# Ordering six of eight experts by token count on the chip, with one overflow loop instead of two

## The chip, the cores and the metric

The kernel runs on one core of a Trainium2 chip. The metric is device time in microseconds (us) of one execution; lower is better. The kernel before took 1444.34 us (median of three runs, 1441.13 to 1444.92).

## What is computed

A two-layer decoder block over 256 tokens of width 1024. Layer 0 is a retention layer with a dense SwiGLU, layer 1 a sparse attention with a mixture of experts. All of the change lies in the mixture and in the sum and norm behind it:

```python
logits = x @ w_router                        # 256 x 8
top_v, top_i = top_k(logits, 2); w = softmax(top_v)
gate = sum(one_hot(top_i, 8) * w[..., None], axis=1)
for e in range(8):                           # D 1024, inner width 3584
    a, b = split(x @ w_in[e], 2)
    out = out + gate[:, e:e+1] * ((silu(a) * b) @ w_out[e])
x = layer_norm(alpha * x + out)
```

The weights are float32. Each expert has 44 MB of them and each is read once, so the eight experts read 352 MB.

## The kernel before, in words

**Weights.** The host lays each expert's weights out as 21 blocks of 2 MB ("slots", 128 rows of 16 KB): 14 of `w_in` (`moe_a`) and 7 of `w_out` (`moe_o`). A slot holds two raws of 1 MB. `load` (from L193) gives each slot a place and issues one transfer on SP's queue: in the ring (eight raws, so four slots), in `more` (one slot) or in `ext` (three). So eight slots, 16 MB, can be on their way or in use. A slot is loaded when the slot that held its place has been used (`release`, `load_next`); the order of the loads is the order of use.

**The order of an expert.** The loop `for e in range(NE)` takes the experts in their order 0 to 7, each in four stages s. A stage multiplies the gathered tokens with its part of `w_in` (`w_in`, matmuls of L1239; four slots, two in stage 3), then does the previous stage's product with `w_out` (`w_out`, matmuls of L1301; two slots, one for stage 3), and then transposes this stage's hidden values (`h_transpose`, L1279). The last `w_out` of an expert so falls into stage 0 of the next one. Behind that stage stands the scatter of the finished expert into X3 (`scatter`, L1343 and L1353), behind stage 1 the transposes of the selection matrix (L1182). Experts 2j and 2j+1 share one selection matrix and one gather (`build_S`, `gather`).

**Groups and the branch.** The tokens of an expert stand in up to 96 places, in three groups of 32 (NG = 3). Groups 0 and 1 are always multiplied (`first`). Group 2 is multiplied only if the expert has more than 64 tokens:

```python
with tc.If(M["n", e] > 64) as cmp:
    for j in (i, i + 1):
        mm(j, us[j][1], (2,))
```

Otherwise `zero` (L1226) clears the bank with four small matmuls, five times per expert: once in each stage's `w_in` and once in the first `w_out`. In this text an expert with group 2 is heavy, one without is light. The count is read into a register of the matmul engine by `count`.

**The end.** Behind the last `h_transpose`, `sum_open` (L1385) starts the last sum: four matmuls with the identity bring X3 into four PSUM banks. Then come the last `w_out`, the split of its result on ACT and DVE (L1327, L1328), the scatter matmuls (L1343) and the norm with the output (`last_out`). `gbr`, the norm's factors, is loaded behind the last weights. For more than 96 tokens of an expert there are two overflow loops (`overflow`, L1448), for places 97 to 224 and from 225; on these inputs both loops run no round, so only their reads of the trip count and their branches are executed.

**Names that the change touches.** `M["rg"]` holds rank and gate of each token by expert, `M["cni"]` and `M["cnf"]` the counts as integers and as floats, `C` a table from the host, `zb` a tile of zeros, `bank(tag)` one of four PSUM banks of the tag "mm" or of "acc".

Of the kernel before, what the change touches and what calls it, by code (L numbers as in the profile page):

```python
# [37 lines left out]
LOOK = 3  # L38


def _tables():
    c = np.zeros((128, 1056), np.float32)
# [65 lines left out]
def tile_decoder(ctx, tc, x, ret_w_in, ret_gn_g, ret_w_out, nsa_w_kv, cmp_k_pe, cmp_k_w1, cmp_k_w2,  # L108
# [17 lines left out]
    C = sb.tile([128, 1056 - 384], F32, name="C")  # L126
# [66 lines left out]
    def load(z):  # L193
# [11 lines left out]
        for i, r in enumerate(z.raws):  # L205
            r.ap = ap[:, i * 2048:(i + 1) * 2048]
            for view, src in r.parts:
                nc.sync.dma_start(view(r.ap), src)
# [858 lines left out]
    if stop not in ("r1", "r2", "r3"):  # L1067
# [64 lines left out]
        def moe_gates():  # L1132
# [13 lines left out]
            trip = sb.tile([128, 2], I32, name="trip")  # L1146
            for i in range(2):
                nc.vector.tensor_scalar(trip[:, i:i + 1], mc, cap + i * 128 + 0.5, float(NE), op0=ALU.is_gt,
                                        op1=ALU.mult)
            M["trip"] = trip  # L1150

        def build_S(j):
# [5 lines left out]
            rg = M["rg"]  # L1158
# [52 lines left out]

        def units_m(w, e, i, n):

            us = []
            for j in range(0, n, 2):
                rs = [raw() for _ in range(2)]
                Slot(rs, w[e, (i + j) // 2])
                us.extend([Unit(r, lambda a: a, conv=False) for _ in range(2)] for r in rs)
            return us
# [4 lines left out]
        def zero(ps):  # L1224
            for q in range(4):
                nc.tensor.matmul(ps[q * 32:(q + 1) * 32], zb[:, 0:32], zb, start=True, stop=True,  # L1226
                                 skip_group_check=True)
# [43 lines left out]
        def h_transpose(s):  # L1271
            def f():
                nch = ws(s) // 128
                hT = ptile([128, NG, 2, 128], F32, "hT")
                for gs, tag in (((0, 1), "acc"), ((2,), "mm")):
# [14 lines left out]
        def w_out(e, s, us):  # L1290
# [41 lines left out]
            for i, u in enumerate(us):  # L1332
                step([u[0]], first(i, u[0]), look=0)
                if i % 2:
# [71 lines left out]
        zb = sb.tile([128, 512], BF16, name="zb")  # L1406
# [8 lines left out]
        for e in range(NE):  # L1415
            step([], count(e), look=0)
            for s in range(4):
                nl, nb = (8, 4) if s < 3 else (4, 2)
                w_in(e, s, units_m(wst['moe_a'], e, 8 * s, nl))
                if prev:  # L1420
                    w_out(*prev)
                step([], h_transpose(s), look=0)
                if s == 0:
                    step([], transpose_S(e) if e == 0 else scatter(e - 1), look=0)
                    if e == 0:
                        step([], moe_gates, look=0)
                if s == 1 and e:
# [8 lines left out]
        step([], sum_open, look=0)  # L1436
# [9 lines left out]
        def overflow(i):  # L1446

            n = nc.values_load(M["trip"][0:1, i:i + 1], min_val=0, max_val=NE)  # L1448
            open_phase("over")
            with tc.For_i(0, n, 1) as ev:  # L1450
                col = ptile([128, 2, NT, 1], F32, "ocol")
                nc.vector.tensor_copy(col, M["rg"][:, :, :, bass.ds(ev, 1)])
                nc.vector.tensor_scalar(col[:, 0], col[:, 0], -float(cap + 128 * i), None, op0=ALU.add)
                xf = ptile([128, NT, D], F32, "oxf")
                nc.vector.tensor_add(xf, M["xh"].bitcast(F32), M["xl"].bitcast(F32))
                Sm = ptile([128, NT, 128], F32, "oS")
                for t in range(NT):
                    nc.vector.tensor_scalar(Sm[:, t], iota1, col[:, 0, t], None, op0=ALU.is_equal)
                ps = bank()
                for t in range(NT):  # L1460
                    nc.tensor.transpose(ps[:, tsl[t]], Sm[:, t], ident)
                SmT = ptile([128, S], F32, "oST")
                nc.scalar.copy(SmT, ps[:, 0:256])
                xg = ptile([128, KD, 128], F32, "oxg")
                for kq in range(2):
                    ps = bank()
                    for k in range(4):
                        kk = kq * 4 + k
                        for t in range(NT):
                            nc.tensor.matmul(ps[:, k * 128:(k + 1) * 128], xf[:, t, kk * 128:(kk + 1) * 128],  # L1470
                                             Sm[:, t], start=k == 0 and t == 0, stop=t == 1, skip_group_check=True)
                    nc.scalar.copy(xg[:, kq * 4:kq * 4 + 4], ps.rearrange("p (k n) -> p k n", k=4))
                y = [bank("acc") for _ in range(2)]
                wi_e = moe_w_in[0, bass.ds(ev, 1)].rearrange("o (k p) n -> p (o k) n", p=128)
                wo_e = moe_w_out[0, bass.ds(ev, 1)].rearrange("o (c p) n -> p (o c) n", p=128)
                for g in range(FFE // 256):
                    ab = bank()
# [160 lines left out]
```

## Time and profile before

| | |
|---|---|
| median of three runs | 1444.34 us (1441.13 to 1444.92) |
| the profiled execution's own time | 1444.41 us |
| its span in the trace | 1442.5 us |
| matmul engine (PE) busy | 1354.2 us, 94% |
| vector engine (DVE), scalar engine (ACT) | 471.3 us (33%), 346.8 us (24%) |
| moved by transfers | 450.78 MB, mean 313 GB/s |
| mean granted clock of PE | 0.982 of 2.4 GHz |

A profile shows one execution. PE is the matmul engine and PEld its weight loads, DVE, ACT and POOL are the vector, scalar and general engines, SP issues the transfers. A letter q behind an engine means its sequencer. "L1239" is a line of the kernel. A line of the timeline gives start, duration, engine, line, operation, output and inputs, how many instructions are merged (x), and in brackets the idle time before with what ended it. A float32 matmul shows as two records. The mixture's weights stream from about 600 us to the end, so the last 840 us of the span are the stage that counts here.

### The profile page before, as it was taken

Reading aid. Unit: us, or ns where it says so; the run is one execution under the profiler, and the core shown is the slowest. Engines: PE = TensorE matmul, PEld = TensorE weight load, DVE = VectorE, ACT = ScalarE, POOL = GpSimd, SP = SyncE. Lnnn points to the kernel's source line nnn. Section 1 sums busy time; section 2 is a strip of 40 time slices with the busy share of each in tenths; the row PEclk is TensorE's granted clock in tenths of the full one; section 3 lists DMA queues with packets and bytes.
Section 4 is the critical chain, followed back from the end, with each engine's and each line's share of the span. In section 5 each row is a group of like instructions: output and inputs, shape, how many; then the busy total and the mean of one; then the engine's idle time right before and its main releaser. Section 6 shows DMA issues by size and latency. Waiting matters only on the chain. (4 is left out here: it accounts for less than half of the span.)

```text
span 1442.5 us, 25322 instructions
## 1 busy us (share of the span) xinstructions
PE 1354.2 (94%) x11073; PEld 777.8 (54%) x11073; DVE 471.3 (33%) x845; ACT 346.8 (24%) x653; POOL 62.7 (4%) x74
## 2 busy tenths in 40 slices
PE   8999999999999898899999999989999998879995
PEld 7888878999977657534334333333333343223341
DVE  5756776455574886100100100101001101001002
ACT  4433434444544563200100101011001010000002
POOL 3101101000011100200000000000000000000000
PEclk9999999999999999799999999999999999999997
DMA  9736444555444305899999999999999999999960
GB/s 386 270 137 228 152 186 145 198 203 192 176 152 149 144 1 214 330 426 424 426 426 425 426 425 424 426 424 426 426 426 426 426 425 426 425 425 426 425 269 33
DMA packets 39829, 450.78 MB, mean 313 GB/s; under 512 B 4544, under 2 KB 4704, under 8 KB 7952
## 3 DMA queue, kind: packets, MB, share of 16 engines
q1 hardware_dynamic: 38016, 443.76, 75.1%
q0 software_dynamic: 1536, 4.98, 1.0%
q8 instruction: 108, 1.77, 0.5%
q14 instruction: 25, 0.20, 0.0%
q10 hardware_dynamic: 144, 0.07, 0.0%
HBM read 447.74 MB, written 1.05 MB: 311 GB/s over the span
## 5 line engine op out<-in xcount | busy, mean ns | idle before, releaser
L1239 PE MATMUL mm<-ring,xg 128*32 128x512 f32 (+1 forms) x2336 | 235.8, 554 | 9.9 <-DMA ring<-w_moe_a_dram 5.9
L1263 DVE TENSOR_TENSOR msh<-msh,mm 128x256 f32<-128x256 f32 (+1 forms) x96 | 35.4, 386 | 501.2 <-ACT msh L1262 501.2
L248 DVE TENSOR_TENSOR wlo<-ring,whi 128x1024 fp32r<-128x1024 f32 (+2 forms) x162 | 187.7, 1208 | 32.4 <-ACT whi L247 32.1
L1239 PE MATMUL mm<-ext,xg 128*32 128x512 f32 (+1 forms) x1888 | 182.8, 536 | 6.0 <-DMA ext<-w_moe_a_dram 3.0
L1239 PEld LDWEIGHTS mm<-ring,xg 128*32 128x32 f32 x2336 | 77.7, 111 | 157.9 <-issue 133.6
L247 ACT CAST whi<-ring 128x1024 fp32r<-128x1024 f32 (+2 forms) x162 | 153.7, 1008 | 18.9 <-PE acc L257 12.2
L1262 ACT ACTIVATE msh<-mm 128x256 f32<-128x256 f32 (+1 forms) x96 | 32.2, 356 | 485.4 <-PE mm L1239 485.4
L381 PE MATMUL mm<-xTh,whi 128*128 128x256 f32 x448 | 126.7, 283 | 1.6 <-ACT whi L247 1.6
L1239 PEld LDWEIGHTS mm<-ext,xg 128*32 128x32 f32 x1888 | 66.3, 111 | 114.7 <-issue 93.9
L383 PE MATMUL mm<-xTh,wlo 128*128 128x256 f32 x448 | 126.3, 282 | 0.8 <-DVE wlo L248 0.8
L1301 PE MATMUL acc<-ring,hT 128*32 128x512 f32 x1040 | 119.2, 600 | 7.5 <-DMA ring<-w_moe_o_dram 6.5
L382 PE MATMUL mm<-xTl,whi 128*128 128x256 f32 x448 | 126.1, 281 | 0.0
L1301 PE MATMUL acc<-ext,hT 128*32 128x512 f32 x848 | 94.9, 593 | 4.5 <-DMA ext<-w_moe_o_dram 4.2
L381 PEld LDWEIGHTS mm<-xTh,whi 128*128 128x128 f32 x448 | 84.9, 189 | 2.9 <-ACT whi L247 1.9
L383 PEld LDWEIGHTS mm<-xTh,wlo 128*128 128x128 f32 x448 | 85.0, 190 | 1.0 <-DVE wlo L248 1.0
L382 PEld LDWEIGHTS mm<-xTl,whi 128*128 128x128 f32 x448 | 85.0, 190 | 0.8
L1286 DVE COPY hT<-mm 128x256 f32<-128x256 f32 (+1 forms) x32 | 12.4, 389 | 215.7 <-PE mm L1279 215.7
L1301 PEld LDWEIGHTS acc<-ring,hT 128*32 128x32 f32 x1040 | 36.8, 111 | 82.2 <-issue 70.1
L1284 ACT COPY hT<-acc 128x512 f32<-128x512 f32 (+1 forms) x32 | 17.1, 535 | 223.1 <-PE acc L1279 146.9
L1239 PE MATMUL mm<-more,xg 128*32 128x512 f32 (+1 forms) x640 | 63.2, 541 | 3.8 <-DMA more<-w_moe_a_dram 2.5
L1301 PEld LDWEIGHTS acc<-ext,hT 128*32 128x32 f32 x848 | 29.2, 110 | 65.5 <-issue 56.2
L255 PE MATMUL mm<-whi,xTh 128*128 128x512 f32 (+1 forms) x144 | 55.7, 387 | 0.3 <-ACT xTh L260 0.2
(325 smaller groups left out, 1669.7 us busy)
## 6 DMA issues: line engine op xcount, KB each, us to landing
ring<-w_moe_a_dram SPq DMA_DIRECT2D x55, 2048.0 KB, 27.2
ext<-w_moe_a_dram SPq DMA_DIRECT2D x42, 2048.0 KB, 27.7
ring<-w_moe_o_dram SPq DMA_DIRECT2D x29, 2048.0 KB, 27.7
ext<-w_moe_o_dram SPq DMA_DIRECT2D x21, 2048.0 KB, 27.2
more<-w_moe_a_dram SPq DMA_DIRECT2D x15, 2048.0 KB, 28.5
ring<-w_ffn_b_dram SPq DMA_DIRECT2D x22, 1024.0 KB, 5.8
ring<-w_ret_a_dram SPq DMA_DIRECT2D x16, 1024.0 KB, 8.6
more<-w_moe_o_dram SPq DMA_DIRECT2D x6, 2048.0 KB, 26.5
```

Source lines behind the costliest of these rows:

```text
L247: nc.scalar.copy(u.hi, v)
L248: nc.vector.tensor_sub(u.lo, v, u.hi.bitcast(F32))
L255: nc.tensor.matmul(ps, xh, wh, start=start, stop=False, skip_group_check=True)
L381: nc.tensor.matmul(ps, u.hi[:, k], xh[:, k], start=start and k == 0, stop=False, skip_group_check=True)
L382: nc.tensor.matmul(ps, u.hi[:, k], xl[:, k], start=False, stop=False, skip_group_check=True)
L383: nc.tensor.matmul(ps, u.lo[:, k], xh[:, k], start=False, stop=k == KD - 1, skip_group_check=True)
L1239: nc.tensor.matmul(M["A", g][j * 32:(j + 1) * 32, :n], M["xg", e // 2][:, k, e % 2, g * 32:(g + 1) * 32], v[:, kk, j], start=k == 0, stop= ...
L1262: nc.scalar.activation(sh[:, g, :w], M["A", g][:, :w], AF.Silu)
L1263: nc.vector.tensor_mul(sh[:, g, :w], sh[:, g, :w], M["A", g][:, w:2 * w])
L1284: nc.scalar.copy(dst, src)
L1286: nc.vector.tensor_copy(dst, src)
L1301: nc.tensor.matmul(M["y", g][q:q + 32], hT[0][:, g, cc, j * 32:(j + 1) * 32], v[:, c, h], start=s == 0 and i == 0, stop=s == 3 and i == 1, ...
```

## The change

1. A new step `moe_order`, after the gates of expert 0, ranks the experts on DVE: experts 0 and 1 keep places 0 and 1 (FIXED), the other six are ranked by token count. Rank r goes to the place that PLACES names: places 2 to 7 get ranks 3, 4, 7, 5, 6, 2 (rank 7 has most tokens, rank 2 fewest). The step writes the permutation and the permuted counts (`perm`) and permuted ranks and gates (`rgp`).
2. The weight loads of places 2 to 7 take the expert from a register of SP, which is read from `perm` once per place (`block`). The rest of the kernel works on places instead of experts.
3. The last slot of `moe_o` becomes two slots of one raw.
4. `sum_open` is split into four calls, which stand between the matmuls of stage 2's `w_out` of the last place. The last `h_transpose` takes both its banks from "acc".
5. `zero` multiplies the 32 zero columns with a broadcast of ones, and `zb` shrinks from 512 to 32 columns.
6. The two overflow loops become one, whose body does both parts.

```diff
--- before.py
+++ after.py
@@ -36,10 +36,14 @@
 NEXT = 3
 NHL = 6
 LOOK = 3
+FIXED = 2
+
+PLACES = [0, 1, 3, 4, 7, 5, 6, 2]
 
 
 def _tables():
-    c = np.zeros((128, 1056), np.float32)
+    c = np.zeros((128, 1064), np.float32)
+    c[:, 1054:1062] = PLACES
     i = np.arange(128)
     c[:, 0:128] = np.eye(128)
     c[:, 128:256] = i[:, None] < i[None, :]
@@ -123,7 +127,7 @@
     xr = x[0].rearrange("(t p) d -> p t d", p=128)
     for t in range(NT):
         nc.sync.dma_start(X[:, t], xr[:, t])
-    C = sb.tile([128, 1056 - 384], F32, name="C")
+    C = sb.tile([128, 1064 - 384], F32, name="C")
     iota1 = C[:, 542:670]
     identb = sb.tile([128, 128], BF16, name="identb")
     maskb = sb.tile([128, 2, 128], BF16, name="maskb")
@@ -205,7 +209,7 @@
         for i, r in enumerate(z.raws):
             r.ap = ap[:, i * 2048:(i + 1) * 2048]
             for view, src in r.parts:
-                nc.sync.dma_start(view(r.ap), src)
+                nc.sync.dma_start(view(r.ap), src() if callable(src) else src)
 
     def load_next(kind="raw"):
         i = state["loaded"]
@@ -1143,11 +1147,37 @@
             nc.gpsimd.tensor_scalar(X3, X3, ALPHA, None, op0=ALU.mult)
             mc = ptile([128, 1], F32, "mc", lv=0)
             nc.vector.tensor_reduce(mc, M["cnf"], axis=AX.X, op=ALU.max)
-            trip = sb.tile([128, 2], I32, name="trip")
-            for i in range(2):
-                nc.vector.tensor_scalar(trip[:, i:i + 1], mc, cap + i * 128 + 0.5, float(NE), op0=ALU.is_gt,
-                                        op1=ALU.mult)
+            trip = sb.tile([128, 1], I32, name="trip")
+            nc.vector.tensor_scalar(trip, mc, cap + 0.5, float(NE), op0=ALU.is_gt, op1=ALU.mult)
             M["trip"] = trip
+
+        def moe_order():
+
+            rg, cnf, iota = M["rg"], M["cnf"], C[:, 0:8]
+            key = ptile([128, 8], F32, "okey", lv=0)
+            nc.vector.scalar_tensor_tensor(key, cnf, float(NE), iota, op0=ALU.mult, op1=ALU.add)
+            nc.vector.tensor_scalar(key[:, 0:FIXED], iota[:, 0:FIXED], -float(FIXED), None, op0=ALU.add)
+            w = ptile([128, 4, 8, 8], F32, "ygb")
+            pm = ptile([128, 8, 8], F32, "opm", lv=0)
+            rk = ptile([128, 8], F32, "ork", lv=0)
+            nc.vector.tensor_tensor(pm, key[:, None, :].to_broadcast([128, 8, 8]),
+                                    key[:, :, None].to_broadcast([128, 8, 8]), op=ALU.is_lt)
+            nc.vector.tensor_reduce(rk, pm, axis=AX.X, op=ALU.add)
+            nc.vector.tensor_tensor(pm, C[:, 670:678, None].to_broadcast([128, 8, 8]),
+                                    rk[:, None, :].to_broadcast([128, 8, 8]), op=ALU.is_equal)
+
+            v = ptile([128, 2, 8], F32, "ov8", lv=0)
+            for i, a in enumerate((iota, cnf)):
+                nc.vector.tensor_mul(w[:, i], pm, a[:, None, :].to_broadcast([128, 8, 8]))
+            nc.vector.tensor_reduce(v, w[:, 0:2], axis=AX.X, op=ALU.add)
+            perm = sb.tile([128, 2, 8], I32, name="perm")
+            nc.vector.tensor_copy(perm, v)
+            M["perm"], M["cni"] = perm[:, 0], perm[:, 1]
+            rgp = sb.tile([128, 2, NT, 8], F32, name="rgp")
+            nc.vector.tensor_mul(w, rg.rearrange("p i t e -> p (i t) e")[:, :, None, :].to_broadcast([128, 4, 8, 8]),
+                                 pm[:, None].to_broadcast([128, 4, 8, 8]))
+            nc.vector.tensor_reduce(rgp.rearrange("p i t e -> p (i t) e"), w, axis=AX.X, op=ALU.add)
+            M["rgp"] = rgp
 
         def build_S(j):
 
@@ -1155,7 +1185,7 @@
             if cap < NS:
                 nc.vector.tensor_scalar(sp, iota1[:, None, None, :NS].to_broadcast([128, NT, 2, NS]), 0.0, None,
                                         op0=ALU.mult)
-            rg = M["rg"]
+            rg = M["rgp"] if j else M["rg"]
             for t in range(NT):
                 for i in range(2):
                     e = 2 * j + i
@@ -1209,12 +1239,29 @@
                                            skip_runtime_bounds_check_because="each of the S tokens counts at most once")
             return f
 
+        def block(w, e, i):
+
+            if e < FIXED:
+                return w[e, i]
+
+            def src():
+                if ("w", e) not in M:
+                    M["w", e] = nc.values_load(M["perm"][0:1, e:e + 1], engines=[mybir.EngineType.SP], min_val=FIXED,
+                                               max_val=NE - 1,
+                                               skip_runtime_bounds_check_because="a permutation of the experts")
+                return w[bass.ds(M["w", e], 1), i].rearrange("o p n -> (o p) n")
+            return src
+
         def units_m(w, e, i, n):
 
             us = []
             for j in range(0, n, 2):
-                rs = [raw() for _ in range(2)]
-                Slot(rs, w[e, (i + j) // 2])
+                if e == NE - 1 and w is wst['moe_o'] and i == 12:
+                    src = block(w, e, 6)
+                    rs = [raw((whole(2048), lambda z=z: src()[:, z * 2048:(z + 1) * 2048])) for z in range(2)]
+                else:
+                    rs = [raw() for _ in range(2)]
+                    Slot(rs, block(w, e, (i + j) // 2))
                 us.extend([Unit(r, lambda a: a, conv=False) for _ in range(2)] for r in rs)
             return us
 
@@ -1223,8 +1270,8 @@
 
         def zero(ps):
             for q in range(4):
-                nc.tensor.matmul(ps[q * 32:(q + 1) * 32], zb[:, 0:32], zb, start=True, stop=True,
-                                 skip_group_check=True)
+                nc.tensor.matmul(ps[q * 32:(q + 1) * 32], zb, onesb[:, None, :].to_broadcast([128, 4, 128]), start=True,
+                                 stop=True, skip_group_check=True)
 
         def w_in(e, s, us):
 
@@ -1268,11 +1315,11 @@
                 if i % 2:
                     step([v[1] for v in us[i - 1:i + 1]], lambda i=i: rest(i - 1), look=0)
 
-        def h_transpose(s):
+        def h_transpose(s, last):
             def f():
                 nch = ws(s) // 128
                 hT = ptile([128, NG, 2, 128], F32, "hT")
-                for gs, tag in (((0, 1), "acc"), ((2,), "mm")):
+                for gs, tag in (((0, 1), "acc"), ((2,), last)):
                     ps = bank(tag)
                     for i, g in enumerate(gs):
                         for c in range(nch):
@@ -1287,7 +1334,7 @@
                 M["hT"] = hT
             return f
 
-        def w_out(e, s, us):
+        def w_out(e, s, us, between=None):
 
             hT = {}
 
@@ -1331,6 +1378,8 @@
 
             for i, u in enumerate(us):
                 step([u[0]], first(i, u[0]), look=0)
+                if between:
+                    step([], lambda i=i: between(i // 2, i % 2), look=0)
                 if i % 2:
                     step([v[1] for v in us[i - 1:i + 1]], lambda i=i: rest(i - 1), look=0)
 
@@ -1350,7 +1399,7 @@
                     scatter_mm(e, t, ps, True)
                     for h in range(2):
                         sl = slice(h * 512, (h + 1) * 512)
-                        nc.vector.scalar_tensor_tensor(X3[:, t, sl], ps[h], M["rg"][:, 1, t, e:e + 1], X3[:, t, sl],
+                        nc.vector.scalar_tensor_tensor(X3[:, t, sl], ps[h], M["rgp"][:, 1, t, e:e + 1], X3[:, t, sl],
                                                        op0=ALU.mult, op1=ALU.add)
             return f
 
@@ -1372,18 +1421,16 @@
             ps = bank("mm")
             for g in range(NG):
                 for t in range(NT):
-                    nc.tensor.matmul(ps[:, g:g + 1], M["S4"][:, t, g], M["rg"][:, 1, t, NE - 1:NE],
+                    nc.tensor.matmul(ps[:, g:g + 1], M["S4"][:, t, g], M["rgp"][:, 1, t, NE - 1:NE],
                                      start=g == 0 and t == 0, stop=t == 1, skip_group_check=True)
             M["gs"] = ptile([128, NG], F32, "gs")
             nc.vector.tensor_copy(M["gs"], ps[:, 0:NG])
 
-        def sum_open():
-
-            for t in range(NT):
-                M["z", t] = [bank("mm") for _ in range(2)]
-                for i in range(2):
-                    nc.tensor.matmul(M["z", t][i], ident, X3[:, t, i * 512:(i + 1) * 512], start=True, stop=False,
-                                     skip_group_check=True)
+        def sum_open(t, i):
+
+            ps = bank("mm")
+            M["z", t] = M["z", t] + [ps] if i else [ps]
+            nc.tensor.matmul(ps, ident, X3[:, t, i * 512:(i + 1) * 512], start=True, stop=False, skip_group_check=True)
 
         def last_out():
 
@@ -1403,7 +1450,7 @@
                     nc.scalar.copy(X3[:, t, i * 512:(i + 1) * 512], M["z", t][i])
 
         NS, NG = 96, 3
-        zb = sb.tile([128, 512], BF16, name="zb")
+        zb = sb.tile([128, 32], BF16, name="zb")
         step([], moe_more, look=0)
         step([], moe_ln0, look=0)
         step([], moe_ln1, look=0)
@@ -1417,13 +1464,15 @@
             for s in range(4):
                 nl, nb = (8, 4) if s < 3 else (4, 2)
                 w_in(e, s, units_m(wst['moe_a'], e, 8 * s, nl))
+                tail = e == NE - 1 and s == 3
                 if prev:
-                    w_out(*prev)
-                step([], h_transpose(s), look=0)
+                    w_out(*prev, between=sum_open if tail else None)
+                step([], h_transpose(s, "acc" if tail else "mm"), look=0)
                 if s == 0:
                     step([], transpose_S(e) if e == 0 else scatter(e - 1), look=0)
                     if e == 0:
                         step([], moe_gates, look=0)
+                        step([], moe_order, look=0)
                 if s == 1 and e:
                     step([], transpose_S(e), look=0)
                 if s == 2 and e % 2 and e < NE - 1:
@@ -1433,7 +1482,6 @@
                 if s == 2 and e == NE - 1:
                     step([], slot_gates, look=0)
                 prev = e, s, units_m(wst['moe_o'], e, 4 * s, nb)
-        step([], sum_open, look=0)
         w_out(*prev)
         gbr = raw(*[(lambda a, i=i: a[:, i * D:(i + 1) * D],
                      bass.AP(tensor=v.tensor, offset=v[1, 1].offset, ap=[[0, 128], [1, D]]))
@@ -1443,69 +1491,70 @@
         step([gbu], last_out)
         step([], close_phase)
 
-        def overflow(i):
-
-            n = nc.values_load(M["trip"][0:1, i:i + 1], min_val=0, max_val=NE)
+        def overflow():
+
+            n = nc.values_load(M["trip"][0:1, 0:1], min_val=0, max_val=NE)
             open_phase("over")
             with tc.For_i(0, n, 1) as ev:
...
+                for i in range(2):
...
-        for i in range(2):
-            step([], lambda i=i: overflow(i))
+        step([], overflow)
```

## Rows read from the trace of the kernel before

**Rows 1.** The page: span, PE's granted clock and the transfers in 40 slices.

```profile
span 1442.5 us, 25322 instructions
...
PEclk9999999999999999799999999999999999999997
DMA  9736444555444305899999999999999999999960
```

**Rows 2.** Chain of waits, in order of time: start, us, engine, line.

```profile
1412.07 0.37 PE acc L1279 x2
...
1412.54 3.44 PE mm L1385 x8
1415.98 5.33 PE acc L1301 x48
...
1430.26 0.72 DVE ygb L322
```

**Rows 3.** Stretches, the instructions of L1226 alone; the eight stretches follow the experts.

```profile
1190.00:1290.00 100.00, 2.02 (x20) 0.61 (x20) 0.98 1.01 425
1290.00:1425.00 135.00, 0.00 (x0) 0.00 (x0) 0.99 0.77 325
```

**Rows 4.** Waits of PE, 1191 to 1300 us: total, times, longest.

```profile
PE mm L1239 <- DMA ring<-w_moe_a_dram: 5.4, 4, 2.2
PE acc L1301 <- DMA ring<-w_moe_o_dram: 4.6, 3, 2.1
PE acc L1301 <- DMA ext<-w_moe_o_dram: 3.4, 3, 1.3
PE mm L1239 <- DMA more<-w_moe_a_dram: 1.3, 1, 1.3
PE mm L1239 <- DMA ext<-w_moe_a_dram: 0.8, 2, 0.5
...
PE acc L1182 <- ACT hT L1284: 0.6, 1, 0.6
```

**Rows 5.** Timeline of PE in expert 6.

```profile
1205.69 5.34 PE L1239 MATMUL mm<-ring,xg 128*32 128x512 f32 x32 [2.20 <-DMA ring<-w_moe_a_dram]
...
1222.45 3.64 PE L1239 MATMUL mm<-more,xg 128*32 128x512 f32 x32 [0.18 <-PEq L1252]
...
1290.58 5.34 PE L1301 MATMUL acc<-ring,hT 128*32 128x512 f32 x32 [2.12 <-DMA ring<-w_moe_o_dram]
```

**Rows 6.** Stretches: busy us of PE, PEld, DVE, ACT, POOL; clock, DMA share, GB/s.

```profile
1205.00:1211.00 6.00, 5.31 (x36) 1.54 (x40) 0.35 (x1) 0.38 (x1) 0.00 (x0) 0.72 1.01 426
...
1235.00:1290.00 55.00, 43.21 (x446) 15.71 (x446) 3.09 (x9) 3.81 (x10) 0.96 (x2) 1.00 1.01 425
```

**Rows 7.** The last two weight loads: SP's timeline, and us to landing.

```profile
1368.69 0.33 SPq L204 DMA_DIRECT2D ext<-w_moe_o_dram  x1
...
ext<-w_moe_o_dram SPq DMA_DIRECT2D x1, 2048.0 KB, 26.3
...
1373.84 0.33 SPq L204 DMA_DIRECT2D ring<-w_moe_o_dram  x1
...
ring<-w_moe_o_dram SPq DMA_DIRECT2D x1, 2048.0 KB, 26.1
```

**Rows 8.** Timeline of the end, ACT and DVE.

```profile
1418.76 0.69 ACT L1327 ACTIVATE yhl<-acc,gs 128x512 fp32r<-128x512 f32 x1 [5.86 <-PE acc L1301]
...
1419.48 1.61 DVE L1328 SCALAR_TENSOR_TENSOR yhl<-acc,gs,yhl 128x512 fp32r<-128x512 f32 x2 [6.61 <-ACT yhl L1327]
...
1423.39 1.30 DVE L308 BATCH_NORM_STATS2 st<-mm 128x6 f32<-128x512 f32 x2 [0.59 <-PE mm L1343]
```

**Rows 9.** SP's sequencer at L1448, and at L1450 from 1438 us: ns min/median/max.

```profile
L1448 SPq TENSOR_LOAD <-trip x2: 283/480/677, 1431.5 to 1438.2; - x2
...
L1450 SPq COMPARE_BRANCH  x4: 33/36/41, 1438.1 to 1440.8; - x4
```

**Rows 10.** Timeline of DVE behind the gates of expert 0.

```profile
625.75 0.42 DVE L1263 TENSOR_TENSOR msh<-msh,mm 128x256 f32<-128x256 f32 x1 [11.10 <-ACT msh L1262]
```

More of the change, by code (lines that the diff above doesn't have):

```diff
@@ new lines, in overflow @@
+                for i in range(2):
+                    col = ptile([128, 2, NT, 1], F32, "ocol")
+                    nc.vector.tensor_copy(col, M["rg"][:, :, :, bass.ds(ev, 1)])
+                    nc.vector.tensor_scalar(col[:, 0], col[:, 0], -float(cap + 128 * i), None, op0=ALU.add)
+                    xf = ptile([128, NT, D], F32, "oxf")
+                    nc.vector.tensor_add(xf, M["xh"].bitcast(F32), M["xl"].bitcast(F32))
+                    Sm = ptile([128, NT, 128], F32, "oS")
+                    for t in range(NT):
+                        nc.vector.tensor_scalar(Sm[:, t], iota1, col[:, 0, t], None, op0=ALU.is_equal)
+                    ps = bank()
+                    for t in range(NT):
+                        nc.tensor.transpose(ps[:, tsl[t]], Sm[:, t], ident)
+                    SmT = ptile([128, S], F32, "oST")
+                    nc.scalar.copy(SmT, ps[:, 0:256])
+                    xg = ptile([128, KD, 128], F32, "oxg")
+                    for kq in range(2):
+                        ps = bank()
+                        for k in range(4):
+                            kk = kq * 4 + k
+                            for t in range(NT):
+                                nc.tensor.matmul(ps[:, k * 128:(k + 1) * 128], xf[:, t, kk * 128:(kk + 1) * 128],
+                                                 Sm[:, t], start=k == 0 and t == 0, stop=t == 1, skip_group_check=True)
+                        nc.scalar.copy(xg[:, kq * 4:kq * 4 + 4], ps.rearrange("p (k n) -> p k n", k=4))
+                    y = [bank("acc") for _ in range(2)]
+                    wi_e = moe_w_in[0, bass.ds(ev, 1)].rearrange("o (k p) n -> p (o k) n", p=128)
+                    wo_e = moe_w_out[0, bass.ds(ev, 1)].rearrange("o (c p) n -> p (o c) n", p=128)
+                    for g in range(FFE // 256):
+                        ab = bank()
+                        for z in range(2):
+                            w = ptile([128, KD, 256], F32, "ow", bufs=3)
+                            nc.sync.dma_start(w, wi_e[:, :, z * FFE + g * 256:z * FFE + (g + 1) * 256])
+                            for k in range(KD):
+                                nc.tensor.matmul(ab[:, z * 256:(z + 1) * 256], xg[:, k], w[:, k],
+                                                 start=z == 0 and k == 0, stop=k == KD - 1, skip_group_check=True)
+                        hh = ptile([128, 256], F32, "oh")
+                        nc.scalar.activation(hh, ab[:, 0:256], AF.Silu)
+                        nc.vector.tensor_mul(hh, hh, ab[:, 256:512])
+                        ps = bank()
+                        for c in range(2):
+                            nc.tensor.transpose(ps[:, c * 128:(c + 1) * 128], hh[:, c * 128:(c + 1) * 128], ident)
+                        hT = ptile([128, 2, 128], F32, "ohT")
+                        nc.scalar.copy(hT, ps[:, 0:256].rearrange("p (c n) -> p c n", c=2))
+                        w = ptile([128, 2, D], F32, "ow", bufs=3)
+                        nc.sync.dma_start(w, wo_e[:, 2 * g:2 * g + 2])
+                        for c in range(2):
+                            for i in range(2):
+                                nc.tensor.matmul(y[i], hT[:, c], w[:, c, i * 512:(i + 1) * 512],
+                                                 start=g == 0 and c == 0, stop=g == 13 and c == 1,
+                                                 skip_group_check=True)
+                    ys = ptile([128, D], F32, "oy")
+                    for i in range(2):
+                        nc.scalar.copy(ys[:, i * 512:(i + 1) * 512], y[i])
+                    for t in range(NT):
+                        for i in range(2):
+                            sl = slice(i * 512, (i + 1) * 512)
+                            ps = bank()
+                            nc.tensor.matmul(ps, SmT[:, tsl[t]], ys[:, sl], start=True, stop=True)
+                            nc.vector.scalar_tensor_tensor(X3[:, t, sl], ps, col[:, 1, t], X3[:, t, sl],
+                                                           op0=ALU.mult, op1=ALU.add)
@@ L1514, in overflow @@
             close_phase()
-        for i in range(2):
-            step([], lambda i=i: overflow(i))
+        step([], overflow)
     open_side("split")
```

55 lines of the change are left out of this document (removed).

## The prediction

> **What bounds the kernel now.** I read the page first. The transfer line [rows 1] stands at 9 from the 18th to the 38th slice: the weights of the mixture stream at the rate of all transfer engines until shortly before the end, 425 to 426 GB/s [rows 6], and PE is granted full clock nearly throughout. So two things are near their limit, and the share of busy time doesn't say which one ends last. The chain of waits does [rows 2]: its last piece of weight work is the 5.33 us of the last `w_out`, and between there and the last load nothing but PE stands in it. PE ends that work at 1421.3 us, while the last weights were issued at 1373.84 and landed 26.1 us later, at 1399.9 [rows 7]. PE is 21.4 us behind its loads at the end.
>
> It was not behind all the time. The line of `zero` alone, cut by experts, tells which experts are heavy [rows 3]: 20 records (five times four) are a light one, none a heavy one. The rows shown are experts 6 and 7; the six before them read 20, 0, 20, 20, 0 and 20. So 1, 4 and 7 are heavy, and 7 is the last. In expert 6, which is light, PE waits for loads 13 times, 15.5 us together [rows 4], up to 2.2 us at a time [rows 5]. A light expert leaves PE idle, a heavy one makes it late, and the lateness of the last one is never worked off. The reader should see these two facts side by side: idle PE in expert 6, and loads that lie ready in expert 7.
>
> **The order.** Places 0 to 5 come out as now: light, heavy, light, light, heavy, light, since of experts 2 to 7 two are heavy (4 and 7, ranks 6 and 7) and the ranks of the places are 3, 4, 7, 5, 6, 2. Place 6 becomes heavy and place 7 light. So the work from 1191.2 us, the start of expert 6, has the same sum in another order.
>
> PE's bound: what goes is the waiting. Of the 15.5 us, 0.17 us per wait is the gap that a slot has anyway (0.18 at the row of 1222.45 [rows 5]), 13 x 0.17 = 2.2, which leaves 13.3. Behind the two longest waits 32 matmuls took 5.34 us instead of 3.64 [rows 5], at a granted clock of 0.72 [rows 6], between the two levels of 1.2 and 2.4 GHz: 2 x 1.7 = 3.4. Together 16.7 us. A heavy place 6 takes 5.33 us for a slot of 48 records, as the last one does [rows 2], and a light one 3.81 with its gap; a load takes 4.92 (2.097 MB at 426 GB/s). So hardly a wait is left in place 6, and place 7 works off at 1.1 us per slot what place 6 was late. The end of PE's work is then not before 1421.3 - 16.7 = 1404.6, plus 0.6 for a new wait: the last `h_transpose` has one free "acc" bank for both its parts and waits for ACT's copy, as the transposes of L1182 do now for 0.6 us [rows 4]. That is 1405.2.
>
> The loads' bound: the sum of bytes and the rate stay, so the last load lands at 1399.9 again, and the slot before it at 1368.69 + 26.3 = 1395.0 [rows 7]. Behind that one PE has a light slot (3.81), two of the four opened sums (half of 3.44 [rows 2], 1.72), the transposes with their wait (0.37 for two of the three [rows 2], so 0.5, + 0.6) and 32 light records of the last `w_out` (two thirds of 5.33, 3.5): 1405.2. Both bounds fall together. Since landings vary by about a microsecond (26.3 and 26.1 us here for the same bytes, waits of up to 2.2), I add 0.8 and take 1406.0: 15.3 us earlier than 1421.3. Bounds: 1405.2 below; above 1409.0, if three or four landings are as late as the two long waits.
>
> **The other parts.** *Splitting the last slot* gives nothing: PE comes to it at about 1401.7 and all of it has landed by 1399.9. Without that cover it would be half a load, 2.5 us. *Opening the sum between the loads* moves 3.44 us of PE; only if the loads are the bound does it save 1.7 of them, and that is in the sum above.
>
> *Behind PE's end* the light case is slower. Now groups 0 and 1 are read out while group 2 is multiplied; group 0 is done after 24 of the 48 records, at 1418.65, and ACT begins at 1418.76, long before PE ends [rows 8]. In a light place groups 0 and 1 are the last: group 0 is done 8 records or 0.9 us before PE's end, ACT begins 0.8 before it, DVE 0.7 later (1418.76 to 1419.48), at 0.1 before the end; three groups of 0.80 follow (1.61 for two [rows 8]), then the scatter and the norm 0.6 later (the idle time at 1423.39): 2.9 us behind PE's end against 2.1 now (1421.3 to 1423.39). That costs 0.8. Bounds: 0 and 1.6 (two more groups of DVE).
>
> *One overflow loop.* SP's second read of the trip count stands at 1438.2 and the last branch at 1440.8 [rows 9], the end of the chain there; this stretch of 2.7 us goes. Bounds: 0 if one longer jump costs as much as two; 6.3 if the first loop's long gap (the first read at 1431.5, 6.7 us before the second) shrinks too. I take 2.7, as the first loop keeps its form.
>
> *`moe_order`* is 11 small DVE instructions. Nearest rows give 0.15 to 0.42 us each, so 1.7 to 4.6 us, and DVE is idle for 11.1 us right there [rows 10]. Without that cover it would delay the first stage by up to 4.6 us. *SP* reads one register for each of six places, 0.3 to 0.7 us [rows 9], and issues 126 loads with an address from it. No row shows such a load on this queue. From below its issue costs the 0.33 us of now [rows 7]; from above it matters only beyond the 4.92 us from load to load, as 26 us of transfers lie ahead of it in the queue. I take 0. The permutation is ready in expert 0, and the first such load stands at most eight slots of 4.92 us ahead of place 2, so SP doesn't wait for it; behind it on SP stand only weight loads. *`zero`* keeps its count; if reading a broadcast were dearer, the last place's five would cost up to 2.0 us (20 records in 2.02 [rows 3]) if they doubled; the rows give no reason for it, 0. The smaller clear of `zb` saves at most 0.2 us; 0.
>
> **Sum.** -15.3 + 0.8 - 2.7 = -17.2 us. The profiled execution took 1444.41 us around its span of 1442.5, and stands 0.07 us from the median, so 1427.2 us.
>
> **A rule weighed.** After the two waits over 2 us the clock was at 0.72, and in the stretch from 1235 to 1290, with waits of 0.3 to 1.5 us, it stayed at 1.00 [rows 6]. The Trainium skill ("TensorE: Matmul & The Clock Gate", HAM oscillation) says that a matmul engine that waits for its loads falls back to the slow clock and begins the next tile cold, which speaks against putting the light expert last, where waits are never worked off. By that rule each long wait near the end costs 1.7 us again. The trace agrees for the long waits and not for the short ones; a sum with two of them would be 3.4 higher.
>
> **Rivals.** *The clock at the end*: the light last place catches up with its loads, two waits grow over 2 us, and each is followed by 32 matmuls at half clock: 2 x (1.7 + 1 for the wait itself beyond the jitter) = 5.4 us, 1432.6. For it: the waits of expert 6 repeat over 2 us twice. Against: by my steps place 7 comes to its loads only at the very end. 0.12. *Slower*: loads with an address from a register hold up the stream. It decides if the 126 of them take on average more than 4.92 + 17.2/126 = 5.06 us each; at 5.2 us they cost 35 us, 1462. For it: no row shows one. Against: SP is idle for over 4 us of each 4.92. 0.07. *The order gives nothing*, since PE's total work were the bound in any order: only the loop's 2.7 remain, 1441.7. The waits of [rows 4] speak against it. 0.05. *More*: the first loop's gap goes as well, and no landing jitters: 1444.4 - 16.1 + 0.8 - 6.3, about 1423. 0.10. The forecast, 0.66, lies within 1424 to 1431.
>
> The range that holds 8 in 10 takes in the clock and the larger gain: 1422 to 1435. Faster by over 0.3% (4.3 us, about what a measurement of this kernel can tell from no change) are the forecast, the clock and the larger gain, 0.88; within it lies the order that gives nothing, 0.05; slower 0.07.
>
> **What would show it.** Right: no `zero` in place 6 and 20 records in place 7; PE's waits for loads from 1191 to 1300 under 3 us; PE's last weight work near 1406; loads still landing at 1399.9 with the transfer share at 1.0; one read of the trip count per engine. Wrong: a transfer share under 1.0 between 700 and 1380, SP waiting or busy for over 4 us per load, a clock under 0.8 in the last 20 us of PE's work, or more than 4 us between PE's end and the norm.

## The result, and the profile after

The changed kernel takes 1426.68 us (median of four runs, 1425.14 to 1427.42) against 1444.21 before on the same chip (a fourth run has moved its median from 1444.34): a ratio of 0.9881, 95% interval 0.9863 to 0.9899, so 1.2% faster, 17.2 us by the ratio and 17.5 by the medians. Forecast were 1427.2 us and a range of 1422 to 1435. The profiled execution took 1426.39 us, with a span of 1424.6.

The page of the changed kernel, with the lines that answer to [rows 1]:

```profile
span 1424.6 us, 25498 instructions
...
PEclk9999999999999999799999999999999999999998
DMA  9736453555544403799999999999999999999992
```

The transfer line stands at 9 nearly to the end: the stream of weights is as long as before, and what stood behind it has become short. The chain of waits of the changed kernel, in order of time, says the same in pieces:

```profile
1402.72 3.62 PE acc L1348 x32
...
1406.36 0.69 ACT yhl L1374
...
1407.08 0.76 DVE yhl L1375
...
1409.08 1.29 DVE st L312 x2
```

The last weight work has 32 records instead of 48 [rows 2] and ends at 1406.34 instead of 1421.3, 15.0 us earlier. The norm begins 2.7 us behind it instead of 2.1, which costs 0.7; and from there to the end of the span it is 15.5 us instead of 19.1, 3.6 less. The three add up to 17.9, the difference of the spans.

That the heavy expert moved is seen in the line of `zero` alone (L1273 now), in the stretches of places 6 and 7:

```profile
1190.00:1300.00 110.00, 0.00 (x0) 0.00 (x0) 1.00 1.01 426
1300.00:1425.00 125.00, 2.11 (x20) 0.69 (x20) 0.96 0.77 324
```

Place 6 has none and place 7 has 20, the reverse of [rows 3]. The waits of PE in the changed kernel from 1190 to 1410 us:

```profile
PE acc L1348 <- DMA ext<-w_moe_o_dram: 1.8, 1, 1.8
...
PE acc L1326 <- ACT hT L1331: 0.5, 1, 0.5
PE mm L1286 <- DMA ext<-w_moe_a_dram: 0.5, 1, 0.5
```

Of the 15.5 us in 13 waits [rows 4], 2.3 us in two are left, both in the last 25 us of PE's weight work. The loads themselves did not get faster. The last whole slot and the second half of the last one, us from issue to landing (issued at 1362.37 and 1366.76):

```profile
ext<-w_moe_o_dram SPq DMA_DIRECT2D x1, 2048.0 KB, 31.8
...
ring<-w_moe_o_dram SPq DMA_DIRECT2D x1, 1024.0 KB, 32.4
```

They landed at 1394.2 and 1399.2, within a microsecond of 1395.0 and 1399.9 before [rows 7], though they were issued 6 to 7 us earlier. PE was 21.4 us behind its loads at the end and is now 7.1 behind.

### The profile page after: what moved, and what is told of

It reads as the page before. It is cut to its first block, busy times and chain, and to the rows that moved or that the text cites. A ratio compares the mean times of both kernels' runs of the same rounds, so it can differ in the third digit from the quotient of the medians.

```text
span 1424.6 us, 25498 instructions
## 1 busy us (share of the span) xinstructions
PE 1350.9 (95%) x11073; PEld 778.9 (55%) x11073; DVE 473.5 (33%) x855; ACT 346.8 (24%) x653; POOL 62.7 (4%) x74
## 5 line engine op out<-in xcount | busy, mean ns | idle before, releaser
L251 ACT CAST whi<-ring 128x1024 fp32r<-128x1024 f32 (+2 forms) x162 | 153.7, 1008 | 18.5 <-PE acc L261 11.8
L1348 PE MATMUL acc<-ext,hT 128*32 128x512 f32 x864 | 98.5, 602 | 5.4 <-DMA ext<-w_moe_o_dram 4.9
## 6 DMA issues: line engine op xcount, KB each, us to landing
ext<-w_moe_a_dram SPq DMA_DIRECT2D x42, 2048.0 KB, 25.3
ring<-w_moe_o_dram SPq DMA_DIRECT2D x28, 2048.0 KB, 25.3
```

Source lines behind the costliest of these rows:

```text
L251: nc.scalar.copy(u.hi, v)
L1348: nc.tensor.matmul(M["y", g][q:q + 32], hT[0][:, g, cc, j * 32:(j + 1) * 32], v[:, c, h], start=s == 0 and i == 0, stop=s == 3 and i == 1, ...
```

## The experiments

The executions of one kernel differ by up to 8.5 us (the kernel before, 1440.53 to 1448.99 on one chip), and part of that is made before the mixture's stream begins. The table therefore cuts each profile at three marks: I, the first load that SP issues once PE works on the mixture; E, the end of PE's last weight work; N, the start of the norm. The median is that of the timed runs.

| kernel | I | E | E - I | N - E | span end - N | median us |
|---|---|---|---|---|---|---|
| before | 596.86 | 1421.31 | 824.5 | 2.1 | 19.1 | 1444.21 |
| changed | 596.73 | 1406.34 | 809.6 | 2.7 | 15.5 | 1426.68 |
| e1, heavy last | 596.51 | 1420.58 | 824.1 | 2.1 | 15.7 | 1441.00 |
| e2, order only | 594.61 | 1403.48 | 808.9 | 2.8 | 18.5 | 1427.58 |
| e3, one loop only | 601.20 | 1423.79 | 822.6 | 2.1 | 15.7 | 1438.93 |
| e4, sum late | 596.59 | 1404.63 | 808.0 | 2.8 | 15.3 | 1424.90 |
| e5, fixed addresses | 599.19 | 1408.67 | 809.5 | 2.8 | 15.7 | 1426.97 |
| e6, last slot whole | 594.76 | 1403.52 | 808.8 | 2.8 | 15.6 | 1426.42 |
| e7, heavy ones early | 595.07 | 1404.60 | 809.5 | 2.8 | 15.5 | 1426.63 |
| e8, heavy ones in a row | 598.68 | 1433.57 | 834.9 | 2.8 | 16.0 | 1453.43 |
| e9, sum in the waits | 596.11 | 1402.57 | 806.5 | 2.7 | 16.3 | 1423.37 |
| e10, changed again | 596.34 | 1405.22 | 808.9 | 2.8 | 15.2 | 1427.59 |

The two profiles of the changed kernel differ by 0.7 us in E - I, and before, e1 and e3, which end on the heavy expert, by up to 1.9; differences of that size tell nothing by themselves. Between those three and the kernels with the new order, e8 apart, lie 13 to 18 us.

**e1: all edits, but the heavy expert last.**

```diff
-PLACES = [0, 1, 3, 4, 7, 5, 6, 2]
+PLACES = [0, 1, 3, 4, 6, 5, 2, 7]
```

> PLACES is [0, 1, 3, 4, 6, 5, 2, 7]: the changed kernel with all its edits, but the expert with most tokens in place 7, the one with fewest in place 6; light and heavy follow each other as before the change. Theory (the order itself gives the 15 us, by filling PE's waits for loads of place 6): PE's last weight work ends near 1421 again, PE waits about 15 us for loads between 1191 and 1300, the span is about 1439 (before less 2.8 for the loop and 0.7 for the end), about 1441 us. Rival (the loads from a register, the opened sum or the smaller tail give the gain): it stays within 3 us of the changed kernel, at 1424 to 1430.

Measured: 1441.00 us, a ratio to before of 0.9982 (0.9967 to 0.9997). E - I is 824.1, as before. PE's timeline has its waits back, 16 for loads with 17.3 us together from 1191 to 1300; two of them:

```profile
1204.08 3.64 PE L1286 MATMUL mm<-ring,xg 128*32 128x512 f32 x32 [1.89 <-DMA ring<-w_moe_a_dram]
...
1288.87 3.64 PE L1348 MATMUL acc<-ring,hT 128*32 128x512 f32 x32 [1.80 <-DMA ring<-w_moe_o_dram]
```

This kernel still loads by a register, opens the sum between the loads and has one loop. With light and heavy exchanged in places 6 and 7 the 15 us are gone: the order makes them, and the 3.4 us that stay stand behind the norm, where the one loop is.

**e2: the order, with the small `zb` that it needs.**

```diff
 # the kernel before, with
+step([], moe_order, look=0)
+src = w[bass.ds(M["w", e], 1), i]          # places 2 to 7
 # and M["perm"], M["rgp"], the small zb with its zero; last slot, sum_open and the two loops as before
```

> The kernel before with only the order on the chip (moe_order, loads by a register, permuted counts and gates; zb small, since the permuted gates need its room): last slot whole, sum opened behind the last transposes, two overflow loops. Theory: PE's weight work ends within 1 us of the changed kernel's 1406.3, the norm follows 2.7 later, and both loops stand at the end: about 3.5 slower than the changed kernel, 1430. Rival (the opened sum and the split of the last slot are needed to reach the loads' bound): 1.7 to 4.2 us more than that, 1432 to 1434.

Measured: 1427.58 us, 0.9888 (0.9863 to 0.9913). E - I is 808.9, no worse than the changed kernel's 809.6 and 808.9, and the end behind N has the two loops again, 18.5. It came out 2.4 us under the expected 1430; its profiled execution had I 2.1 us earlier, which is no part of the change (the I of its other executions is not known). The opened sum and the split slot are not needed for the gain.

**e3: one loop and nothing else.**

```diff
-        for i in range(2):
-            step([], lambda i=i: overflow(i))
+        step([], overflow)          # its body does both parts
```

> The kernel before with only the two overflow loops made one. Theory as predicted: the stretch from the second read of the trip count to the last branch goes, 2.7 to 2.8 us, and 0.7 more between the last branch and the end of the span, as in the changed kernel: 1440.7. Rival (one longer jump costs as much as two): 1444.

Measured: 1438.93 us, 0.9972 (0.9956 to 0.9987), so 1.9 to 6.4 us faster than before. The stretch from the norm to the span's end is 15.7 against 19.1 us: 3.4 less. The profiled execution was a late one (I at 601.20). One longer jump does not cost as much as two.

**e4: the sum opened late again.**

```diff
-                    w_out(*prev, between=sum_open if tail else None)
-                step([], h_transpose(s, "acc" if tail else "mm"), look=0)
+                    w_out(*prev)
+                step([], h_transpose(s, "mm"), look=0)
 ...
+        step([], sum_open, look=0)
         w_out(*prev)
```

> The changed kernel with the sum opened in one piece behind the last transposes, as before, and these again on two tags. As predicted (opening between the loads saves 1.7 of 3.4 us, the wait for the one bank costs 0.6): 1.1 us slower than the changed kernel. By the changed kernel's timeline instead (its slot landed at 1394.2 and PE came to it at 1395.4; late opening would leave PE idle for about 1 us before that slot, but saves the wait for ACT's copy and comes to the last slot at 1402.0 instead of 1402.65): 0.7 us faster, 1426.

Measured: 1424.90 us, 0.9870 (0.9847 to 0.9894). Its interval overlaps that of the changed kernel, so the medians decide nothing, and neither does E - I: 808.0 here and 808.9 in e2, whose sum is late too, against 809.6 and 808.9. It depends on when the first of the last two whole slots of `w_out` lands: PE's first matmul on it comes 791.8 to 792.7 us behind I. From that matmul to E it is 16.2 us in e4 and in e2, and 16.9 to 17.0 in all five profiles with the sum opened between the loads (changed, e10, e5, e6, e7). So the late sum isn't 1.1 us slower, as my prediction had it, but 0.7 faster, as the second of the two expectations had it. That first matmul in e2 and in e10:

```profile
1387.29 3.64 PE L1346 MATMUL acc<-ext,hT 128*32 128x512 f32 x32 [1.12 <-DMA ext<-w_moe_o_dram]
```

```profile
1388.28 1.92 PE L1348 MATMUL acc<-ext,hT 128*32 128x512 f32 x16 [1.21 <-DMA ext<-w_moe_o_dram]
```

PE's timeline of e4:

```profile
1388.43 3.64 PE L1348 MATMUL acc<-ext,hT 128*32 128x512 f32 x32 [1.10 <-DMA ext<-w_moe_o_dram]
1393.24 3.64 PE L1348 MATMUL acc<-ext,hT 128*32 128x512 f32 x32 [1.17 <-DMA ext<-w_moe_o_dram]
...
1400.94 3.64 PE L1348 MATMUL acc<-ring,hT 128*32 128x512 f32 x32
```

and of the changed kernel:

```profile
1389.39 1.92 PE L1348 MATMUL acc<-ext,hT 128*32 128x512 f32 x16 [1.84 <-DMA ext<-w_moe_o_dram]
...
1395.43 1.92 PE L1348 MATMUL acc<-ext,hT 128*32 128x512 f32 x16
...
1402.39 0.33 PE L1326 MATMUL acc<-ident,msh 128*128 128x128 f32 x1 [0.51 <-ACT hT L1331]
1402.65 3.64 PE L1348 MATMUL acc<-ring,hT 128*32 128x512 f32 x32
```

In e4 PE stands twice for 1.1 us before a slot. In the changed kernel the first two sums come behind the first half slot and behind the second, so PE still waits 1.84 us before the first slot (1.21 in e10), and then comes to the second at 1395.4, 1.2 us after its landing. The sums are not in the waits, they stand in front of a slot that is there already; and the transposes with one bank wait 0.51.

**e5: the same order, with addresses in the program.**

```diff
-                return w[bass.ds(M["w", e], 1), i].rearrange("o p n -> (o p) n")
+            return w[[0, 1, 6, 5, 7, 3, 4, 2][e], i]
```

> The changed kernel with the same order of experts, but the loads' addresses written into the program (experts 0, 1, 6, 5, 7, 3, 4, 2) instead of read from SP's register; moe_order still ranks counts and gates. Theory (an issue costs 0.33 us as before, 0.05 and 0.03 for two register operations, and 26 us of transfers lie ahead): no difference, within 0.7 us. Rival (the register loads delay the stream): faster, by up to 126 x 0.08 = 10 us if each one's operations came on top.

Measured: 1426.97 us, 0.9884 (0.9863 to 0.9905); E - I 809.5. No difference that this can tell. What the register costs is in the changed kernel's rows of SP (the read at L1249, the loads of L208; ns min/median/max):

```profile
L1249 SPq TENSOR_LOAD <-perm x6: 277/278/498, 746.0 to 1263.6; - x6
...
L208 SPq FUSED_REGOPS  x125: 43/46/56, 746.5 to 1358.9; - x125
L208 SPq DMA_DIRECT2D ring<-w_moe_a_dram x55: 327/333/602, 474.6 to 1337.6; - x55
```

A load with an address from the register takes 333 ns to issue, where before and in e5 it takes 327 to 328, and 46 ns for its address (with a move of 29); 4.9 us lie between two loads.

**e6: the last slot whole.**

```diff
-                if e == NE - 1 and w is wst['moe_o'] and i == 12: ...   # two raws of 1 MB
+                rs = [raw() for _ in range(2)]
+                Slot(rs, block(w, e, (i + j) // 2))
```

> The changed kernel with the last slot of w_out whole, one load of 2 MB. Theory (PE comes to it at 1402.65, both halves have landed by 1399.2): no difference, within 0.7 us. Rival (PE or SP gains by the halves): up to 2.5 us slower.

Measured: 1426.42 us, 0.9889 (0.9867 to 0.9911); E - I 808.8. No difference that this can tell.

**e7: heavy experts in places 1, 3 and 5.**

```diff
-PLACES = [0, 1, 3, 4, 7, 5, 6, 2]
+PLACES = [0, 1, 3, 6, 4, 7, 5, 2]
```

> PLACES is [0, 1, 3, 6, 4, 7, 5, 2]: heavy experts in places 1, 3 and 5, so that two light ones end the kernel. Theory (the end is bound by the loads and what follows a landing, the same as in the changed kernel): PE waits for loads in places 6 and 7, its weight work ends within 1 us of 1406.3, the time within 1.5 us of the changed kernel. Rival (the clock: waits over 2 us cool PE before the end): granted clock under 0.9 in the last 20 us of PE's work and 2 to 6 us slower.

Measured: 1426.63 us, 0.9890 (0.9867 to 0.9914); E - I 809.5. With two light places at the end PE waits again, but no longer than 1.3 us at a time, and the clock stays. Stretches of e7 (PE, PEld, DVE, ACT, POOL, clock, transfer share, GB/s):

```profile
1320.00:1360.00 40.00, 34.25 (x308) 10.72 (x308) 3.48 (x7) 2.49 (x6) 0.00 (x0) 1.00 1.01 426
1360.00:1380.00 20.00, 16.27 (x172) 6.31 (x167) 1.76 (x5) 1.63 (x4) 0.00 (x0) 1.00 1.01 426
```

PE is idle for 14% and 19% of them, and gains nothing by the earlier work: the loads bound the end.

**e8: the three heavy experts in a row.**

```diff
-PLACES = [0, 1, 3, 4, 7, 5, 6, 2]
+PLACES = [0, 1, 7, 6, 3, 4, 5, 2]
```

> PLACES is [0, 1, 7, 6, 3, 4, 5, 2]: the three heavy experts in a row in places 1 to 3, four light ones behind. A heavy place makes PE about 14 us later than its loads, and eight slots hold 39 us of loads. Theory (keeping heavy ones apart is worth something because the slots run out): in place 3 PE is 30 to 40 us late, the transfer share falls below 1.0 there, and the last landing comes 5 to 15 us later: 1431 to 1442. Rival (any order with the lightest last does as well): within 1.5 us of the changed kernel.

Measured: 1453.43 us, 1.0069 (1.0048 to 1.0091): slower than before, though the last expert is the lightest. Stretches of e8:

```profile
640.00:800.00 160.00, 156.75 (x1588) 60.48 (x1592) 14.48 (x35) 13.52 (x33) 1.02 (x2) 1.00 1.01 425
800.00:1040.00 240.00, 237.48 (x2366) 85.28 (x2358) 23.00 (x50) 20.00 (x46) 1.98 (x4) 1.00 0.95 375
1040.00:1390.00 350.00, 306.13 (x2906) 112.45 (x2907) 40.74 (x88) 33.18 (x80) 2.94 (x6) 1.00 1.01 426
```

and the time from issue to landing in 880 to 920 us, of e8 first, then of the changed kernel:

```profile
DMA to landing us min/median/max: 9.2/9.9/10.3
```

```profile
DMA to landing us min/median/max: 29.2/32.3/35.9
```

From place 2 on PE holds so many slots that only about two loads (9.9 us of 4.92 each) are on their way, and a new one starts only when PE gives up a slot. The stream runs at 375 instead of 426 GB/s for 240 us; what it misses, 51 x 240 = 12.2 MB, is 28.7 us at full rate. E - I is 25.3 us over the changed kernel's. The last four places can't make it good: from 1177 us on PE waits for loads again, 36 times, and the loads already run at their rate. I had expected place 3 alone to be hit, and 5 to 15 us; the slots run out in place 2.

**e9: the sum in the waits, and e10: the changed kernel again.**

```diff
+                if tail:
+                    step([], lambda: sum_open(0, 0), look=0)
                 if prev:
                     w_out(*prev, between=sum_open if tail else None)   # only sum_open(0, 1), between the two slots
-                step([], h_transpose(s, "acc" if tail else "mm"), look=0)
+                step([], h_transpose(s, "mm"), look=0)
 ...
+        for i in range(2):
+            step([], lambda i=i: sum_open(1, i), look=0)
         w_out(*prev)
```

> The changed kernel with the opened sum put where PE waits for a load: one call before stage 2's w_out of place 7, one between its two slots, and two behind the last transposes, which go to two tags again. Theory (the loads bound the end: behind the landing of the last whole slot, at 1393.2 in the run with the sum opened late, PE has a light slot, 3.8, transposes, 0.5, the sums still to open and the last w_out, 3.6): the two sums moved into the waits of 1.1 us each save 1.7 against that run, so PE's weight work ends near 1403 and the time is about 2.5 to 3.3 under the changed kernel's, 1423 to 1424. Rival (PE's own work bounds the end in any arrangement): the same as with the sum opened late.

> The changed kernel as it is, beside the one with the sum in the waits: 1426 to 1428, and a second profile, to see how far PE's first matmul of the mixture and the end of its weight work move from one execution to the next; by the other runs 1 to 3 us.

Measured on one chip: e9 1423.37 us, 0.9860 (0.9835 to 0.9885), e10 1427.59 us, 0.9886 (0.9863 to 0.9909). E - I is 806.5 against 808.9, and 808.0 with the sum late. PE's timeline of e9:

```profile
1386.78 1.13 PE L1433 MATMUL mm<-X,ident 128*128 128x512 f32 x2
1388.05 3.64 PE L1348 MATMUL acc<-ext,hT 128*32 128x512 f32 x32
1391.86 1.10 PE L1433 MATMUL mm<-X,ident 128*128 128x512 f32 x2 [0.17 <-PEq L1362]
1392.89 3.64 PE L1348 MATMUL acc<-ext,hT 128*32 128x512 f32 x32
```

Neither slot has a wait before it. By its median this is the fastest kernel of the study. The intervals of the ratios overlap, and so do the runs on this chip (1422.11 to 1426.03 against 1424.37 to 1429.47 for e10); what speaks for it is the cut. From PE's first matmul on the first of the two slots to E it is 14.5 us, 1.7 under e4, as expected, and 2.4 under the changed kernel. Behind N this profile is 1.1 us longer than e10's, 16.3 against 15.2; SP's four issues of the output span 3.73 us there instead of 2.77, and why was not tried.

## Why the prediction was right, point by point

**The order: right in mechanism and size.** PE's weight work was forecast to end at 1406.0 and ended at 1406.34. The waits of place 6 went, PE's and the loads' bounds met at the end, and the last loads landed within a microsecond of where they had before. That the end was met to 0.3 us is in part luck: both bounds stood at 1405.2, and the 0.8 that I had added for late landings had to cover the opened sum as well, which I had counted as a gain; and by e10's E - I the end would have come 0.7 earlier. e1 gives the 15 us back by exchanging light and heavy in places 6 and 7, and e2 has them with only the small `zb` beside the order. The rival that the order gives nothing falls with e1.

**What the prediction took for granted.** The loads' bound held because no two heavy experts stand next to each other. My steps had a rate that stays, and only in passing that 26 us of loads are on their way behind a heavy expert. e8 shows the price of the condition: what made a kernel slower than before was not the register but the supply of slots.

**The slower rival: shown wrong.** Loads by a register cost SP 0.05 to 0.08 us of 4.9, and e5 without them is no faster.

**Behind PE's end.** +0.8 was forecast, +0.7 measured. **One loop: right, but sized too small.** 2.7 us were forecast, 3.6 measured in the changed kernel and 3.4 in e3. The order gave 0.3 us less than forecast, the norm's start 0.1 and the loop 0.9 more: 17.9 in the profiles where 17.2 were forecast. SP has one read instead of two, and three branches:

```profile
L1496 SPq TENSOR_LOAD <-trip x1: 617/617/617, 1417.1 to 1417.1; - x1
...
L1498 SPq COMPARE_BRANCH  x3: 41/43/54, 1418.1 to 1423.6; - x3
```

where the kernel before has six:

```profile
L1450 SPq COMPARE_BRANCH  x6: 33/38/53, 1432.6 to 1440.8; - x6
```

From the first read to the last branch it is 6.5 us instead of 9.3 [rows 9], so 2.8 less where 2.7 were forecast; the rest, 0.7, stands between the last branch and the span's end (1.0 us against 1.7), which I hadn't counted.

**Opening the sum: wrong.** The step that it saves 1.7 us where the loads are the bound failed. By e4 and e2 it costs 0.7 us instead, because its calls stand behind the wait and not in it. e9, with two of the four calls in the waits, shows that the 1.7 us are there to be had.

**The split slot and `moe_order`: right at nothing.** e6 for the one; for the other, DVE's next instruction still begins at 625.70, and the idle time before it has shrunk from 11.1 us [rows 10] to 8.4:

```profile
625.70 0.42 DVE L1310 TENSOR_TENSOR msh<-msh,mm 128x256 f32<-128x256 f32 x1 [8.41 <-ACT msh L1309]
```

**The clock: it did not decide.** In the stretch that the order changes, from 1190 us on, the long waits of [rows 5] are gone and nothing like them came; the longest is 1.84 us. In e7 and e1, with waits up to 1.3 and 1.9 us there, the next 32 matmuls took 3.64 us at full clock. But the rival's price, 1.7 us behind each wait over 2 us, is not a fixed one. A row of the changed kernel in place 3 (where the kernel before has a wait of 2.21 us), one of e3 and one of e8:

```profile
955.57 5.34 PE L1348 MATMUL acc<-ext,hT 128*32 128x512 f32 x32 [2.01 <-DMA ext<-w_moe_o_dram]
```

```profile
1239.79 3.64 PE L1299 MATMUL acc<-ext,hT 128*32 128x512 f32 x32 [2.05 <-DMA ext<-w_moe_o_dram]
```

```profile
1287.65 3.64 PE L1286 MATMUL mm<-more,xg 128*32 128x512 f32 x32 [2.81 <-DMA more<-w_moe_a_dram]
```

Behind the first the 32 matmuls ran slow (granted clock 0.76 from 955 to 962 us, between the levels of 1.2 and 2.4 GHz), behind the two longer ones at full clock (1.00). The length of the wait alone doesn't decide it; what does was not tried. The Trainium skill ("TensorE: Matmul & The Clock Gate", HAM oscillation) tells of a kernel whose waits for loads each let the clock fall, so that the next tile starts cold. The waits of [rows 5] and the first of these rows agree with it, the other two and the shorter waits show no loss.

## What to carry to other kernels

Where a stream of loads and an engine have nearly the same total, look for the stretch in which the engine waits and the one in which it is late, and move work from the second to the first; the buffers between them set how much lateness in a row the stream can bear (here three heavy experts in a row took up the eight slots, and E - I was 25.3 us longer than with them apart, more than the right order gains). End on work that is shorter than its load, but expect then to be bound by the last landing and by what must follow it. Work meant to fill a wait has to be issued ahead of the instruction that waits.

## What the runs showed of the hardware that was not expected

The stream doesn't end at once. Stretches of the changed kernel (the last two columns are transfer share and GB/s):

```profile
1300.00:1380.00 80.00, 77.32 (x703) 28.50 (x699) 10.03 (x21) 7.87 (x18) 0.00 (x0) 1.00 1.01 426
...
1386.00:1393.00 7.00, 5.16 (x58) 1.72 (x50) 0.77 (x3) 0.74 (x3) 0.00 (x0) 1.00 0.53 222
1393.00:1400.00 7.00, 6.85 (x48) 1.64 (x40) 0.00 (x0) 0.00 (x0) 0.00 (x0) 1.00 0.47 192
```

For the last 14 us only half of the transfer time is used, at half the rate, and the last two loads land in that stretch or at its end (1394.2 and 1399.2). The kernel before has the same tail, with shares of 0.55 and 0.48 in the same two stretches. In e8, which has a stretch with few loads on their way, it was about 7 us long. By an estimate, 7 us less of it at half the rate are 3.5 us, about the difference between the 28.7 us that e8's stream missed and the 25.3 by which E - I grew. Where the tail comes from was not tried and stays open; at the full rate its bytes would take 7 us.

Much of the spread between profiles lies ahead of the mixture: in the five with the new order and the sum between the loads (changed, e10, e5, e6, e7) I moved from 594.76 to 599.19 us, and E - I only from 808.8 to 809.6.
